# A hybrid decoder layer on one core: a third quarter-block product in the second map, with sums, residual and a gate on GpSimd

## The chip, the cores and the metric

The kernel runs on one core of a Trainium2 chip. The metric is the device time of one execution in microseconds (us). Engines are called as the profile calls them: PE (TensorE matmul) with PEld (its weight load), DVE (VectorE), ACT (ScalarE), POOL (GpSimd), SP (SyncE, which here only issues DMAs).

## The reference

One layer, in fp32, for a sequence of S = 2048 rows of width 1024 with hidden width 4096 (cut to what matters):

```python
h = x * (1.0 + sc1) + sh1
z = h @ w_in                       # 1024 x 2048
gate_b, gate_c, v_conv, v_pool = split(z)
mix = concat(gate_b * conv3(gate_c * v_conv), pool(v_pool)) @ w_out
x = layer_norm(ALPHA * x + (1.0 + g1) * mix, ln1_g, ln1_b)
h = x * (1.0 + sc2) + sh2
f = square(relu(h @ w_mlp_in)) @ w_mlp_out      # 1024 x 4096, 4096 x 1024
x = layer_norm(ALPHA * x + (1.0 + g2) * f, ln2_g, ln2_b)
```

The vectors sh1 to g2 come from a small product with c. The last two lines, called "second map" (the product with `w_mlp_out`) and "close" here, are where most of the change lies.

## The kernel before

The rows are cut into two blocks of T = 1024 rows. Each block passes through `in_proj`, `out_proj`, eight groups of `up` (the first MLP map, 512 hidden columns each, with squared ReLU), and `down` (the second map with the closing LayerNorm). The next stage's operands are made while the present one multiplies.

**Three passes per product.** fp32 operands are split by `split` (L80): ACT casts to a high part (L81), DVE subtracts it for a low part (L82), and `mm3` (L85) does three matmuls, high x high, high x low, low x high (L86 to L88).

**Seven products for eight.** Each large product is cut into 2 x 2 blocks and done with seven block products (Strassen-Winograd) on sums of blocks. `ORDER` lists the seven: 0 is A11 x B11, 1 is A12 x B21, 2 to 4 use sums on both sides, 5 and 6 a sum on one. The sums of blocks are made by DVE, go to DRAM (`usum`, `w2sum`) and come back as operands.

**`down` of block 2** (`b` = 1, L1082 on). F[0..7] are eight row tiles of 128 rows by 1024 columns of the result. A step is one block product over half of the hidden groups, so two steps make a product. The steps are `coarse = (0, 2, 3, 4, 6)`; each step has 96 matmuls of 128x512. `operands(n)` issues the loads and splits of a step while the step ahead of it runs. Products 1 and 5 are not in the list: they are "fine", that is each is once more cut into seven products of quarter blocks (256 columns wide, L1118), and these 14 follow step 1. The quarter sums come from `save_quarters` (activations, L960, made in `up`) and from `sum_blocks` on `w2q` (weights, `wquart`), both on DVE. Their loads need four transfers of 512 KB per quarter product.

**Order of the work.** A scheduler puts instructions into each engine's queue by the priorities in which the code issues them, and the tiles of a pool (`o` 12 buffers, `h` 28, `r` 5, `w` 6, PSUM `ps` 8 banks) hold a later user back until a buffer is free. GpSimd only issues stores.

**Residual.** `residual()` (L1066) makes ALPHA * ln1_g * n + ALPHA * ln1_b for eight tiles on DVE: load `nsave`, multiply, add, store to `rsave`. In block 2 it starts at step 2 (`base`), two tiles to a step.

**Close.** When a row tile is complete, `first_row` or `second_row` or `last` gates it with g2, adds the residual, and `normalise` does statistics, scale and finish. Product 3 ends the tiles 0 to 3 (`third_row`, where ACT copies PSUM into F), product 4 the right half of the tiles 4 to 7, product 6 their left half, which ends the kernel. The last row tile (F[7], left half) is done in two quarters of 256 columns in one PSUM bank (`cut` in `matmuls`), so that DVE can work on one while PE does the other. `last_part` gates a quarter by a DVE multiply out of PSUM, adds the residual and takes statistics.

**Start of `out_proj` of block 2.** `in_proj_1` ends with `keep` (L628, ACT copies out of PSUM), `conv` (ACT ACTIVATE L325, DVE L326, L327) and `pool_mid` (DVE L261, L265). The first matmuls of `out_proj` write into a PSUM bank that one of the L628 copies must have read.

Of the kernel before, what the change touches and what calls it, by code (L numbers as in the profile page):

```python
# [13 lines left out]
P = 128  # L14
# [17 lines left out]
QUARTER_SUMS = (0, 1, 1, 1, 1, 1, 1, 2)  # L32
# [11 lines left out]
def tile_hybrid_layer(ctx: ExitStack, tc: tile.TileContext, opening, xT, x, wada, vec, win0, win,  # L44
                      wins, wpool, wout, wmix, w1, w2, w2q, rows, out):
# [46 lines left out]


# [88 lines left out]
    uquart = tc.dram_tile([2, 7, 2, P, T], F32, name="uquart")  # L182
    wquart = tc.dram_tile([2, 2, 4, P, T], F32, name="wquart")
# [434 lines left out]

    def in_proj_1(X, W, first_w):
# [13 lines left out]

        def group(j):
# [6 lines left out]
            keep(cut(values, 0), x_)  # L641
            nc.vector.tensor_copy(v[:, :HALO], vhalo[:, j, :])
# [4 lines left out]
            add(cut(values, 0), y_)  # L647
            if j == 0:
                inputs(X, ORDER[4][1])
# [5 lines left out]
            keep(cut(values, 1), x_)  # L655
            if j == 0:
                inputs(X, ORDER[5][1])
            product(3, z_, True)
            keep(cut(gates, 1), z_)
            if j == 0:  # L660
                inputs(X, ORDER[6][1])
# [4 lines left out]
            add(cut(gates, 1), x_)  # L666
            if last:
                ops.begin(1)
            product(5, z_, False)
            add(cut(values, 1), z_)  # L670
            if last:
                ops.weights(0, 1)
                pt = pool_mid(1, j, v)
            product(6, x_, False)
            keep(cut(gates, 0), x_)
            if last:
# [6 lines left out]
            for hs in halves if last else [slice(0, T)]:  # L683
# [4 lines left out]
                if last and hs.start == 0:  # L688
                    mixed.extend([y[:, :H], None, pt[:, :H], pt[:, H:]])
# [267 lines left out]
    FINE = {1: 0, 5: 1}  # L957
    UQ = {"11": 0, "12": 1, "22": 2, "s1": 3, "s2": 4, "s3": 5, "s4": 6}

    def save_quarters(r, n, g):  # L960
        hf, cols = g // 4, slice(g % 4 * Q, g % 4 * Q + Q)
        a11, a21, a12, a22 = (r[:, i * Q : i * Q + Q] for i in range(4))
        q = t_o()
        s1, s2, s3, s4 = (q[:, i * Q : i * Q + Q] for i in range(4))
# [4 lines left out]
        tt(s1, a21, a22, ALU.add)  # L969
        tt(s2, s1, a11, ALU.subtract)  # L970
        tt(s3, a11, a21, ALU.subtract)
        tt(s4, a12, s2, ALU.subtract)
        nc.gpsimd.dma_start(dst[3:7].rearrange("a p n -> p a n"), q.rearrange("p (a n) -> p a n", a=4))

# [3 lines left out]
    def up(g, B, fine):  # L978
# [19 lines left out]

        def save(r, i):
            if fine and i in (1, 7):  # L1000
                save_quarters(r, i // 4, g)
            else:
                nc.gpsimd.dma_start(usum[g, i], r)  # L1003
# [466 lines left out]
```

## Time and profile before

| | |
|---|---|
| median of 3 runs | 1734.32 us (1734.28 to 1735.41) |
| profiled execution | 1734.73 us, span 1733.0 us |
| PE busy | 1720.9 us, 99% |
| PEld busy | 1439.4 us, 83% |
| DVE busy | 1342.6 us, 77% |
| ACT busy | 879.5 us, 51% |
| POOL busy | 235.7 us, 14% |
| granted TensorE clock, mean | 0.999 |

The span runs from the first to the last instruction of the core; the 1.73 us that the profiled execution has beyond it lie outside. A matmul's listed duration is longer than its pitch, since matmuls are pipelined: the distance between starts is what a matmul costs. Idle time of an engine other than PE matters only where PE, or the end, waits for it.

### The profile page before, as it was taken

To read this page: it belongs to the slowest core of one execution; us is meant where nothing else is said; L and a number is where in the kernel's file an instruction comes from. 1 tells how busy PE (TensorE), PEld (TensorE's weight loads), DVE (VectorE), ACT (ScalarE), POOL (GpSimd) and SP (SyncE) were. 2 spreads that over 40 slices of the span, in tenths; PEclk is the share of its full clock that TensorE was granted. 3 is DMA by queue.
4 is the path that set the end of the run, shared out by engine and by line. 5 is a ranking of instruction groups with operands and counts; after the bars stand their busy time and mean duration, and the time that the engine had idled before them with its cause. 6 is when DMAs were issued, how large, how long until landed. Compare 5 with 4: busy or idle time off the path is not lost.

```text
span 1733.0 us, 22349 instructions
## 1 busy us (share of the span) xinstructions
PE 1720.9 (99%) x7998; PEld 1439.4 (83%) x7998; DVE 1342.6 (77%) x1759; ACT 879.5 (51%) x1188; POOL 235.7 (14%) x441
## 2 busy tenths in 40 slices
PE   9999999999999999999999999999999999999997
PEld 8888888888888888888888888888888888998886
DVE  8898798877777676769686779687677768987894
ACT  5323358554454654436573344775444565763451
POOL 0222221122322000000000000103222221000000
PEclk9999999999999999999999999999999999999999
DMA  9899867778888998887572265657655599998871
GB/s 385 343 322 357 321 229 282 280 272 318 327 320 325 366 413 326 303 289 270 190 273 79 104 236 201 218 196 263 248 205 213 201 325 409 417 362 311 285 257 49
DMA packets 149646, 480.47 MB, mean 277 GB/s; under 512 B 17680, under 2 KB 18464, under 8 KB 149536
## 3 DMA queue, kind: packets, MB, share of 16 engines
q1 hardware_dynamic: 102528, 313.87, 49.8%
q0 software_dynamic: 47008, 165.19, 25.0%
q8 instruction: 62, 1.02, 0.2%
q14 instruction: 48, 0.39, 0.1%
HBM read 329.56 MB, written 149.43 MB: 276 GB/s over the span
## 4 chain that ended last, share of the span: by engine, by line
PE 95%; DVE 2%; issue 2%; DMA 1%; ACT 0%; POOL 0%; SPq 0%; DVEq 0%; POOLq 0%; ACTq 0%
PE ps L86 29%; PE ps L87 29%; PE ps L88 29%; PE ps L1118 5%; PE ps L406 3%; PE ps L757 1%; DVE o L91 1%; DMA r<-msum 1%; DMA msum<-o 0%; DMA r<-in_opening 0%; DVE o L1333 0%; DVE o L1339 0%; DVE o L261 0%; DVE st L726 0%; DVE h L82 0%
## 5 line engine op out<-in xcount | busy, mean ns | idle before, releaser
L87 PE MATMUL ps<-h,w 128*128 128x512 f32 x1312 | 510.3, 389 | 0.0
L88 PE MATMUL ps<-h,w 128*128 128x512 f32 x1312 | 510.1, 389 | 0.0
L86 PE MATMUL ps<-h,w 128*128 128x512 f32 x1312 | 510.1, 389 | 0.0
L86 PE MATMUL ps<-h,h 128*128 128x512 f32 (+1 forms) x1000 | 387.9, 388 | 2.2 <-DVE o L91 1.7
L88 PE MATMUL ps<-h,h 128*128 128x512 f32 (+1 forms) x1000 | 387.7, 388 | 0.0
L87 PE MATMUL ps<-h,h 128*128 128x512 f32 (+1 forms) x1000 | 387.5, 387 | 0.0
L81 ACT CAST h<-r 128x1024 fp32r<-128x1024 f32 (+1 forms) x196 | 199.4, 1021 | 279.0 <-PE ps L87 147.5
L82 DVE TENSOR_TENSOR h<-r,h 128x1024 fp32r<-128x1024 f32 (+1 forms) x196 | 230.9, 1182 | 83.4 <-ACT h L81 83.1
L81 ACT CAST w<-r 128x1024 fp32r<-128x1024 f32 x156 | 164.2, 1053 | 257.0 <-PE ps L87 251.2
L87 PEld LDWEIGHTS ps<-h,w 128*128 128x128 f32 x1312 | 246.3, 188 | 51.8 <-DVE h L82 0.5
L88 PEld LDWEIGHTS ps<-h,w 128*128 128x128 f32 x1312 | 246.3, 188 | 51.1
L86 PEld LDWEIGHTS ps<-h,w 128*128 128x128 f32 x1312 | 246.0, 188 | 51.4 <-issue 0.3
L82 DVE TENSOR_TENSOR w<-r,w 128x1024 fp32r<-128x1024 f32 x156 | 190.6, 1222 | 96.5 <-ACT w L81 95.5
L86 PEld LDWEIGHTS ps<-h,h 128*128 128x128 f32 x1000 | 187.8, 188 | 41.3 <-DVE o L91 1.9
L88 PEld LDWEIGHTS ps<-h,h 128*128 128x128 f32 x1000 | 187.8, 188 | 38.5
L87 PEld LDWEIGHTS ps<-h,h 128*128 128x128 f32 x1000 | 187.8, 188 | 38.0
L91 DVE TENSOR_TENSOR o<-o,o 128x1024 f32<-128x1024 f32 (+2 forms) x218 | 186.0, 859 | 42.8 <-DMA usum<-o 39.2
L82 DVE TENSOR_TENSOR h<-w,h 128x1024 fp32r<-128x1024 f32 x124 | 151.2, 1219 | 4.9 <-ACT h L81 4.8
L91 DVE TENSOR_TENSOR o<-o,ps 128x512 f32<-128x512 f32 (+1 forms) x172 | 112.4, 664 | 48.6 <-PE ps L88 48.2
L81 ACT CAST h<-w 128x1024 fp32r<-128x1024 f32 x124 | 130.0, 1049 | 9.5 <-DMA w<-in_w 4.3
L1003 POOL DMA_DIRECT2D usum<-o x96 | 51.7, 538 | 431.9 <-ACT o L997 195.8
L91 DVE TENSOR_TENSOR r<-r,r 128x1024 f32<-128x1024 f32 x60 | 73.4, 1223 | 11.4 <-DMA r<-in_w 7.6
(151 smaller groups left out, 1419.3 us busy)
## 6 DMA issues: line engine op xcount, KB each, us to landing
usum<-o POOLq DMA_DIRECT2D x96, 512.0 KB, 4.2
r<-usum SPq DMA_DIRECT2D x96, 512.0 KB, 5.3
w<-w2sum SPq DMA_DIRECT2D x64, 512.0 KB, 6.1
r<-in_w SPq DMA_DIRECT2D x60, 512.0 KB, 5.8
o<-in_w SPq DMA_DIRECT2D x72, 256.0 KB, 5.8
w2sum<-o POOLq DMA_DIRECT2D x64, 256.0 KB, 6.0
w<-in_w SPq DMA_DIRECT2D x32, 512.0 KB, 6.0
r<-uquart SPq DMA_DIRECT2D x28, 512.0 KB, 9.5
```

Of the source, the lines that this page charges most:

```text
L81: high = nc.scalar.copy(hi, src)
L82: return high.ins, nc.vector.tensor_tensor(lo, src, hi.bitcast(F32), op=ALU.subtract).ins
L86: nc.tensor.matmul(ps, whi, xhi, start=first, stop=False, skip_group_check=goes_on)
L87: nc.tensor.matmul(ps, whi, xlo, start=False, stop=False, skip_group_check=goes_on)
L88: nc.tensor.matmul(ps, wlo, xhi, start=False, stop=last, skip_group_check=goes_on)
L91: return nc.vector.tensor_tensor(out_, a, b_, op=op)
L406: nc.tensor.matmul(ps[m, h], wt[:, w : w + P], A[k][p // 2][:, hs], start=k == 0 and p == 0, stop=k == KD - 1 and p == 2)
L757: nc.tensor.transpose(ps[:, t * P : t * P + P], R[4 * h + t][:, k * P : k * P + P], ident)
L1003: nc.gpsimd.dma_start(usum[g, i], r)
L1118: nc.tensor.matmul(ps, a[:, us], w[:, gs], start=not begun, stop=hf == 1 and g == 3 and a is ul, skip_group_check=True)
```

## The change

- **Third fine product.** Product 0 of block 2's second map leaves `coarse` and becomes seven quarter products, ahead of those of 1 and 5. Product 2 is now the first coarse step and is the one that begins the banks X. Matmuls: 192 fewer of 128x512, 336 more of 128x256. Product 0's result is gathered in the left half of F[4..7], copied by ACT to the right half, and added to F[0..3] by DVE; X is added behind product 5.
- **Operands for it.** The blocks A11 of each group are quartered too (`save_quarters`), for the groups 0 and 1 on GpSimd from a copy that is read back (`again`), for the others on DVE. `save_quarters` now has pauses, and a `Spare` list spreads its pieces between the products of `up`.
- **Weights' quarter sums on GpSimd.** The sums of `w2q`, now of three sets, leave DVE and the end of each `up` group. GpSimd does them in 12 items of four TENSOR_TENSOR 128x512 each, with two loads and four stores on its own queue; four of the items in `in_proj_1`, eight in `up`. The input `w2s` is the same weights laid out for two loads of 128x1024.
- **Residual on GpSimd.** The 16 operations of block 2's residual go from DVE to GpSimd, and begin at step 0: one tile in each of the steps 0 and 1, three in step 2, two in step 3, one in step 4.
- **Product 6 in two.** Its first half ends the banks X. At the start of the second half DVE adds X to F, gates it and adds it to the residual (12 operations of 128x512). The second half runs into fresh banks with weights that GpSimd has multiplied by g2 (8 operations of 128x512), so a tile is closed by one sum (`close.sum`). Each quarter of the last row tile has a PSUM bank of its own.
- **Smaller.** `third_row` adds on DVE where ACT copied. In the last group of `in_proj_1` the pooling step is issued behind both halves' multiplies.

The diff, cut to its core:

```diff
+    def quarter_sums(n, hf, p):
+        a, b_ = t_o(T), t_o(T)
...
+        for i, r in enumerate((a, b_)):
+            nc.gpsimd.dma_start(r, w2s[n, hf, p, i])
+        yield
+        yield
+        gt(b22, b22, b12, ALU.subtract)
+        gt(b12, b12, b11, ALU.subtract)
+        yield
+        gt(b11, b22, b11, ALU.add)
+        gt(b21, b21, b11, ALU.subtract)
...
-                pt = pool_mid(1, j, v)
...
                 if last and hs.start == 0:
+                    pt = pool_mid(1, j, v)
...
-    FINE = {1: 0, 5: 1}
+    FINE = {0: 2, 1: 0, 5: 1}
...
+            for hs in halves if gate is not None else ():
+                nc.gpsimd.tensor_tensor(q[:, hs], q[:, hs], gate, op=ALU.mult)
...
-            tt(r, r, ag, ALU.mult)
-            tt(r, r, ab, ALU.add)
+            op = gt if ends[0] == 0 else tt
+            op(r, r, ag, ALU.mult)
+            op(r, r, ab, ALU.add)
             nc.gpsimd.dma_start(rsave[t], r)
-            if t % 2:
+            if t in ends:
                 yield
...
-        coarse = (0, 2, 3, 4, 6) if b else (0, 1, 2, 3, 5, 4, 6)
+        coarse = (2, 3, 4, 6) if b else (0, 1, 2, 3, 5, 4, 6)
...
             for c in range(0, H if cut else 0, Q):
+                ps = t_ps()
...
-                        mm3(banks[3][:, c : c + Q], uh[:, cs], ul[:, cs], wh[:, ws_], wl[:, ws_],
-                            False, n == len(ops) - 1 and p == 1, True)
-                last_part(slice(c, c + Q), banks[3][:, c : c + Q])
+                        mm3(ps[:, :Q], uh[:, cs], ul[:, cs], wh[:, ws_], wl[:, ws_],
+                            n == p == 0, n == len(ops) - 1 and p == 1)
+                last_part(slice(c, c + Q), ps[:, :Q])
...
         def third_row(t, ps):
-            keep(t + 4, hi_, ps)
+            add(t + 4, hi_, ps)
...
         def last_part(cs, ps):
-            tt(F[7][:, cs], ps, g2[:, cs], ALU.mult)
-            close.add(7, cs, rest[6][3][:, cs])
+            close.sum(7, cs, rest[6][3][:, cs], ps)
...
-        base = 2 if b else 5
+        base, turns = (0, 5) if b else (5, 4)
...
-        later = residual()
+        later = residual((0, 1, 4, 6, 7) if b else (1, 3, 5, 7))
...
+                if b and i == 6:
+                    for t in range(4):
+                        add(t + 4, lo_, X[t])
+                        gate(t + 4, lo_)
+                        tt(rest[6][t], rest[6][t], F[t + 4][:, lo_], ALU.add)
+                    table[6] = Y, True, last
...
+                        if k == 0:
+                            nc.scalar.copy(F[t + 4][:, hi_], F[t + 4][:, lo_])
+                            continue
+                        cs = lo_ if k == 1 else hi_
+                        tt(F[t][:, cs], F[t][:, cs], F[t + 4][:, lo_], ALU.add)
+                        if k == 5:
+                            add(t, hi_, X[t])
...
-            sums = [(sum_blocks, [w2q[n, i, hf] for i in range(4)], wquart[n, hf], p)
-                    for n in range(2) for hf in range(2) for p in halves]
```

Line numbers of the changed kernel differ: its DVE helper is L90 (L91 before), its GpSimd helper L94, a tile's scale L1454 (L1333), its finish L1460 (L1339), a quarter's statistics L1427 (L1309).

**The end of the kernel on DVE.** The rows below stand at the end of DVE's queue, from the scale of the row tile before the last (L1333) to the last tile's statistics; `o_11449` is the last row tile, `ps_11549` its one bank, `bc` the row of g2. Before:

```order
L1333 SCALAR_TENSOR_TENSOR o_14128<-o_11448,mv_14130,w_13402 128x1024
L91 TENSOR_TENSOR o_11449<-ps_11549,bc_4830 128x256
L1339 SCALAR_TENSOR_TENSOR o_14128<-o_14128,mv_14130,w_13404 128x1024
L91 TENSOR_TENSOR o_11449<-o_11449,r_14022 128x256
L1309 BN_STATS st_13789<-o_11449 128x6
```

After, with `o_11543` the last row tile and `r_14365` its residual:

```order
L1454 SCALAR_TENSOR_TENSOR o_14483<-o_11542,mv_14485,w_13732 128x1024
L90 TENSOR_TENSOR o_11543<-r_14365,ps_14496 128x256
L1460 SCALAR_TENSOR_TENSOR o_14483<-o_14483,mv_14485,w_13734 128x1024
L1427 BN_STATS st_14124<-o_11543 128x6
L90 TENSOR_TENSOR o_11543<-r_14365,ps_14523 128x256
L1427 BN_STATS st_14124<-o_11543 128x6
L789 BN_AGGR mv_14551<-st_14124 128x2
```

The multiply by g2 and the separate addition have become one sum from a quarter's own bank (`ps_14496`, `ps_14523`); the scale and the finish of the tile before stand as they did.

**The start of `out_proj` on ACT.** In ACT's queue, where the last group of `in_proj_1` ends; the L628 copies free PSUM banks, L325 is the first step of the convolution of one half. Before:

```order
L628 COPY o_8142<-ps_8059 128x512
L325 ACTIVATE o_8142<-o_8046,vecs 128x512
L628 COPY o_8143<-ps_8072 128x512
L325 ACTIVATE o_8142<-o_8046,vecs 128x512
L81 CAST h_8353<-o_8309 128x512
```

After, where the copies are L676 and the convolution L327:

```order
L676 COPY o_8194<-ps_8111 128x512
L327 ACTIVATE o_8194<-o_8098,vecs 128x512 x2
L676 COPY o_8195<-ps_8124 128x512
L80 CAST h_8395<-o_8413 128x512
L80 CAST h_8390<-o_8194 128x512
```

The second copy now stands behind both ACTIVATEs; these wait for two DVE multiplies, which now stand next to each other in DVE's queue, where a pooling step (L261) stood between them.

**The residual.** Before, in DVE's queue, while product 2's second step ends; `r_13202` and `r_13207` are two residual tiles, the L82 rows are splits of operands:

```order
L91 TENSOR_TENSOR r_13202<-r_13202,o_12884 128x1024
L91 TENSOR_TENSOR o_11445<-o_11445,ps_11549 128x512
L82 TENSOR_TENSOR h_13183<-r_13178,h_13182 128x1024
L82 TENSOR_TENSOR h_13187<-w_13180,h_13186 128x1024
L91 TENSOR_TENSOR r_13202<-r_13202,o_12886 128x1024
L91 TENSOR_TENSOR r_13207<-r_13207,o_12884 128x1024
```

After, the tiles 5 to 7 in POOL's queue, which in this stage holds nothing else:

```order
L94 TENSOR_TENSOR r_13690<-r_13690,o_11640 128x1024
L94 TENSOR_TENSOR r_13690<-r_13690,o_11642 128x1024
L94 TENSOR_TENSOR r_13695<-r_13695,o_11640 128x1024
L1178 DMA rsave<-r_13690 128x1024
L94 TENSOR_TENSOR r_13695<-r_13695,o_11642 128x1024
L1178 DMA rsave<-r_13695 128x1024
L94 TENSOR_TENSOR r_13942<-r_13942,o_11640 128x1024
```

The two operations of each tile and its store are now in one queue, and DVE's queue has the splits without the residual between them.

More of the change, by code (lines that the diff above doesn't have):

```diff
@@ L1033, in up @@
             join(c12, Z)
+            beside_()
+        for item in kept:
+            quarters_beside.finish(item)
         s1 = t_o()
@@ L1047, in up, with down_operands @@
         save(c11, 7)
-    def down_operands(i, gs):
+        beside_()
+        if fine and g == NC - 1:
+            quarters_beside.step(99)
+            sums_beside.step(99)
+    def down_operands(i, gs, gate=None):
         a, w = ORDER[i]
@@ L1064, in down_operands, with residual @@
         return out_, done
-    def residual():
+    def residual(ends):
         ag, ab = row(t_o(D), rows[0]), row(t_o(D), rows[1])
@@ L1123, in quarter_of @@
             c = (H if i == 5 else 0) + col * Q
-            return [F[2 * row + t][:, c : c + Q] for t in range(2)]
+            return [F[(0 if i else 4) + 2 * row + t][:, c : c + Q] for t in range(2)]
         def fine_copy(i, row, col, bank):
@@ L1146, in down, with matmuls @@
         fine_banks = {}
-        def matmuls(banks, ops, new, begins, ends, then, by_tile, cut=False):
+        def matmuls(banks, ops, new, begins, ends, then, by_tile, cut=False, closes=False):
+            begins = begins or cut
             if new and begins:
-                for t in range(4):
+                for t in range(3 if cut else 4):
                     banks[t] = t_ps()
```

135 lines of the change are left out of this document (106 added, 29 removed).

## The prediction

> **What bounds the kernel now.** I read the page's busy times and its chain first, then PE's waits over block 2, then the chain, the timelines and the table by stretches at the places that the change touches. Busy times and the shares of the chain:
>
> ```profile
> PE 1720.9 (99%) x7998; PEld 1439.4 (83%) x7998; DVE 1342.6 (77%) x1759; ACT 879.5 (51%) x1188; POOL 235.7 (14%) x441
> ...
> PE 95%; DVE 2%; issue 2%; DMA 1%; ACT 0%; POOL 0%; SPq 0%; DVEq 0%; POOLq 0%; ACTq 0%
> ```
>
> PE is the bound nearly everywhere, so two things can shorten the time: less matmul work, and the few places where PE stands still. PE's waits from 900 us to the end (line, what it waited for, total, times, longest) are two:
>
> ```profile
> PE ps L86 <- DVE o L91: 1.7, 1, 1.7
> PE ps L86 <- ACT o L628: 0.6, 1, 0.6
> ```
>
> The first lies at the end, the second at the start of `out_proj`. The end, from the timelines of DVE and PE (start, length, what, idle time before):
>
> ```profile
> 1717.20 0.69 DVE L91 TENSOR_TENSOR o<-ps,bc 128x512 f32<-128x512 f32 x1
> 1717.93 0.69 DVE L91 TENSOR_TENSOR o<-o,r 128x512 f32<-128x512 f32 x1
> ...
> 1720.04 1.27 DVE L1333 SCALAR_TENSOR_TENSOR o<-o,mv,w 128x1024 f32<-128x1024 f32 x1
> 1721.22 0.42 DVE L91 TENSOR_TENSOR o<-ps,bc 128x256 f32<-128x256 f32 x1
> ...
> 1724.87 0.42 DVE L91 TENSOR_TENSOR o<-ps,bc 128x256 f32<-128x256 f32 x1 [1.24 <-PE ps L88]
> 1725.32 0.42 DVE L91 TENSOR_TENSOR o<-o,r 128x256 f32<-128x256 f32 x1
> 1725.78 0.43 DVE L1309 BATCH_NORM_STATS2 st<-o 128x6 f32<-128x256 f32 x1
> ```
>
> ```profile
> 1719.76 0.28 PE L88 MATMUL ps<-h,h 128*128 128x256 f32 x1
> 1721.69 0.39 PE L86 MATMUL ps<-h,h 128*128 128x256 f32 x1 [1.66 <-DVE o L91]
> ```
>
> PE's second quarter of the last row tile (1721.69) writes the bank that DVE's multiply at 1721.22 still reads for the first quarter, and that multiply stood behind the scale of the tile before (1720.04). Then DVE waits for PE in turn, and from 1724.87 multiply, add, statistics, scales and finishes run alone to the end.
>
> **PE's work.** A matmul costs its pitch, not its listed length. The chain (start, length, what):
>
> ```profile
> 1400.09 0.23 PE ps L87
> ...
> 1406.21 0.23 PE ps L87
> ...
> 1467.87 80.63 PE ps L1118 x672
> ```
>
> The first two rows are the same line nine groups of three apart: 6.12 / 27 = 0.2267 us for 128x512. The third is the whole fine stage: 80.63 / 672 = 0.120 us for 128x256. The change takes away 192 of the first and adds 7 x 48 = 336 of the second: 336 x 0.120 - 192 x 0.2267 = 40.3 - 43.5 = **-3.2 us**. A half-wide matmul costs 53% of a full one, so seven products for eight (-12.5%) brings 7%.
>
> **The end.** With a bank for each quarter, PE's second quarter follows the first after 0.12 instead of 1721.69 - 1719.76 = 1.93 us: 1.81 less. Its result is then there at 1724.87 - 1.81 = 1723.06. Is DVE free by then? The tile before now has one sum where a multiply and an add stood, so all behind 1717.93 comes 0.73 earlier: its scale ends at 1721.31 - 0.73 = 1720.6; behind it stand quarter one's sum (0.42), the finish (1.27, as long as the scale) and quarter one's statistics (0.43), until 1722.7. It is free, with 0.4 us to spare. The last statistics start one sum of 0.45 later, at 1723.51 instead of 1725.78: **-2.27 us**.
>
> What pays for it are 12 operations of 128x512 on DVE at the start of the last step (add X, gate, add to the residual), 12 x 0.69 = 8.3 us. X's banks close six matmuls (1.36 us) apart, the last with the step's start; each brings 2.1 us of DVE work, so the four run from 4.1 us ahead of the step to 4.3 behind it, and the step's first tile comes after 24 x 0.2267 = 5.44 us. The cover is PE's first tile and an idle DVE (columns: stretch, length, then busy time and count of PE, PEld, DVE, ACT, POOL; clock, DMA share, GB/s):
>
> ```profile
> 1690.00:1712.00 22.00, 22.00 (x98) 18.21 (x97) 5.61 (x10) 1.18 (x4) 0.00 (x0) 1.00 0.00 1
> ```
>
> Without that cover the tiles would start up to 4 us late and regain 0.7 each. GpSimd's gate of the weights stands ahead of four splits in a stretch where DVE has time; I cost it at nothing there.
>
> **The start of `out_proj`.** ACT and DVE:
>
> ```profile
> 1043.89 0.73 ACT L325 ACTIVATE o<-o,vecs 128x512 f32<-128x512 f32 x1 [4.84 <-DVE o L91]
> 1044.52 0.57 ACT L628 COPY o<-ps 128x512 f32<-128x512 f32 x1
> ```
>
> ```profile
> 1042.02 1.23 DVE L261 TENSOR_TENSOR o<-o 128x1033 f32<-128x1033 f32 x1
> 1043.17 0.68 DVE L91 TENSOR_TENSOR o<-o,o 128x512 f32<-128x512 f32 x1
> ```
>
> PE's 0.6 us end with the copy, which stands behind the ACTIVATE, which waits for DVE's second multiply (1043.17) behind a pooling step of 1.23. With the multiplies adjacent that ACTIVATE starts 1.15 us earlier; the copy now stands behind a second one of 0.63 (1044.52 - 1043.89) that was behind it, so it comes about 0.5 earlier: **-0.5 us**, between 0 (the second half's pooling, now later, is waited for in its place) and -0.6.
>
> **DVE, ACT and the loads.** The third fine product is made at the pace of the other two. Two stretches of the fine stage, and the groups of ACT and DVE that feed it (count | busy, mean ns | idle before):
>
> ```profile
> 1468.00:1488.00 20.00, 20.00 (x169) 20.00 (x169) 18.45 (x18) 16.23 (x20) 0.00 (x0) 1.00 1.03 418
> ...
> 1528.00:1548.00 20.00, 20.00 (x169) 20.00 (x169) 17.96 (x19) 14.53 (x16) 0.00 (x0) 1.00 1.01 365
> ```
>
> ```profile
> L81 ACT CAST h<-r 128x1024 fp32r<-128x1024 f32 x28 | 29.5, 1052 | 16.2 <-PE ps L1118 15.6 <-DMA r<-uquart 0.6
> ```
>
> A quarter product takes 48 x 0.120 = 5.76 us and loads 2.1 MB, 364 GB/s; ACT's idle time ends with PE, which frees its buffers, so the preparation waits for PE and not the other way round. PE stayed full for 80 us at this pace, and 121 us are the same state for longer: 0, up to +2 if the 364 GB/s, with the residual's transfers now ahead of the stage, start with fewer buffers filled.
>
> In `up` DVE loses the weights' sums and gains quarter sums of activations. It is at 71% there:
>
> ```profile
> 1250.00:1300.00 50.00, 50.00 (x223) 41.39 (x222) 33.75 (x40) 23.26 (x28) 10.24 (x18) 1.00 0.60 222
> ```
>
> **GpSimd, and product 3.** The trace has no computation on POOL; how long its operations last, and whether they hold up DVE, is the open price. It matters where DVE is full:
>
> ```profile
> 1630.00:1650.00 20.00, 20.00 (x90) 16.57 (x89) 19.89 (x36) 13.28 (x27) 0.00 (x0) 1.00 0.71 239
> 1650.00:1670.00 20.00, 20.00 (x90) 16.57 (x89) 19.23 (x23) 10.89 (x16) 0.00 (x0) 1.00 0.96 349
> ```
>
> ```profile
> L91 DVE TENSOR_TENSOR o<-o,ps 128x512 f32<-128x512 f32 x8 | 5.5, 684 | 3.3 <-PE ps L88 3.2
> ...
> L91 DVE TENSOR_TENSOR r<-r,o 128x1024 f32<-128x1024 f32 x4 | 4.8, 1224 | 6.6 <-DMA r<-nsave 6.6
> ```
>
> ```profile
> 1655.73 1.21 DVE L82 TENSOR_TENSOR h<-w,h 128x1024 fp32r<-128x1024 f32 x1
> ```
>
> ```profile
> 1661.47 0.39 PE L87 MATMUL ps<-h,h 128*128 128x512 f32 x1
> ```
>
> The split that ends at 1656.94 is first used at 1661.47: a lead of 4.5 us, the shortest in this stage. From 1613 us the residual's four operations leave DVE (-4.9 us), `third_row` brings four adds of 0.68 (+2.7): the lead grows to 6.7. In the same stretch POOL now has six operations (residual tiles 5 to 7). If each stops DVE for a time d, PE loses 6d - 6.7 us: 0.6 at d = 1.22 (DVE's own length for the operation), 7.9 at twice that, nothing below 1.1. Some fall where DVE was idle anyway (the 6.6 above), and nothing in the trace shows that they stop DVE at all, so I take 0 and keep +8 for the range.
>
> The Trainium skill speaks against the change here: by "SBUF — State Buffer" (section "SBUF: two separate sides") GpSimd and a DVE operation with two SBUF inputs take one port pair in turn, each for its whole length, and by "GPSIMD Engine Reference" (section "3.1 Elementwise — side-by-side cycle accounting") an addition takes 4497 ns on GpSimd for 2048 elements, half of which, 2.25 us, is an estimate for 1024. By these d = 2.25 and the loss 6.8 us. No trace here shows either.
>
> **Sum.** -3.2 - 2.27 - 0.5 = -6.0. The profiled execution, 1734.73 (span 1733.0 and 1.73 outside it), becomes 1728.8; the median of the runs, 1734.32, lies 0.4 below it and becomes 1728.35. I forecast **1728.5**.
>
> **The rivals.**
> *GpSimd stops DVE for a while* (0.13). For it: DVE at 99% from 1630 on, nearly all of it with two SBUF inputs; against it, the lead of 6.7. With d between 1.5 and 2.7 the loss is 2.3 to 9.5 us and the time 1730.8 to 1738; at twice DVE's length, with two of the six in DVE's idle time, 4 x 2.44 - 6.7 = 3.1, thus 1731.6. This is the rule named above.
> *GpSimd is slow enough to make it slower* (0.12). The same place from d = 2.7 on, by stopping DVE, or because its residual tiles keep two of the five `r` buffers, behind which SP queues the loads of product 4. At three times DVE's length, 3.66, the loss is 15.3 us: 1743.8. For it: the loads and splits of a step have no other way in; against it: these loads are issued a step (96 x 0.2267 = 21.8 us) ahead of use.
> *The end doesn't do what it says* (0.10). DVE is late from the 12 operations, or another wait takes the bank's place. Then the 2.27 go, and with the 0.5 at `out_proj` in doubt too, only PE's 3.2 stay: 1734.32 - 3.2 = 1731.1. For it: only 0.4 us to spare at the last quarter, 1.1 at the first tile.
> *GpSimd's sums hold up `up`* (0.05). Each item takes two of twelve `o` buffers and stands in POOL's queue ahead of the stores that free the others; a late store makes ACT's copies and so PE wait. Against it: POOL is busy 10 of 50 us there. From a delay of some 9 us on; at 0.5 us in each of six groups 1731.5.
>
> **Numbers.** About 0.2%, 3.5 us, is what a measurement of this kernel can tell from no change: faster means below 1730.85, slower above 1737.8. My forecast has 0.60; its own range goes from 1727.3 (the `out_proj` term at 0.6, another 0.45 at the end, half a us of scatter, as 1734.28 to 1735.41 shows) to 1730.5 (+2 in the fine stage). It is faster with nearly all of its weight, and so is a third of the first rival: 0.64. Same: the rest of that rival, the third and the fourth: 0.24. Slower: 0.12. Up to 1735.5 the range holds the forecast, the third and fourth rival and about half of the first: 0.81.
>
> **What would show it.** Right: PE's waits lose both rows; the fine stage is one chain piece of 1008 matmuls, about 121 us long, at the same 0.120; the last statistics start 0.45 us behind PE's last quarter; POOL's operations lie beside DVE's splits without stretching them. Wrong: splits of 128x1024 that last longer than 1.22 us or start late while POOL computes; a wait of PE for DVE or ACT in the second half of product 3 or in product 4; a wait in the fine stage for `uquart` or `wquart`; PE idle in `up` behind ACT's copies; at the end, the first tile's sum behind the 12 operations.

## The result, and the profile after

The changed kernel takes 1766.59 us (median of 4 runs, 1763.7 to 1767.43), beside 1734.3 before (4 runs): a ratio of 1.0182, 95% interval 1.017 to 1.0194. It is 1.8% slower where 0.3% faster was forecast, and far outside the range. The page of the changed kernel, busy times and chain:

```profile
PE 1731.1 (98%) x8142; PEld 1449.5 (82%) x8142; DVE 1412.4 (80%) x1768; ACT 891.5 (51%) x1208; POOL 420.6 (24%) x581
...
PE 72%; DMA 9%; DVE 7%; POOL 4%; issue 4%; ACT 2%; SPq 0%; DVEq 0%; POOLq 0%; ACTq 0%
```

PE's share of the chain has gone from 95% to 72%, and DMA, DVE and POOL have come in. DVE, from which work was to be taken, is busy for 70 us more. PE's waits over the same stretch as in the prediction:

```profile
PE ps L87 <- DVE w L81: 10.6, 5, 4.0
PE ps L86 <- DVE h L81: 7.9, 3, 3.7
PE ps L85 <- ACT h L80: 2.1, 1, 2.1
PE ps L1219 <- ACT o L1229: 0.9, 1, 0.9
PE ps L85 <- DVE o L90: 0.6, 1, 0.6
PE ps L85 <- ACT o L676: 0.2, 1, 0.2
```

Both old waits have gone or shrunk (the 1.7 at the end, and 0.2 is left of the 0.6 at `out_proj`), and eleven new ones have come, eight of them for DVE's splits (L81). The quarter products mark the places (first and last start), in before and in after:

```profile
L1118 PE MATMUL ps<-h,h x672: 277/283/283, 1467.7 to 1548.2; 128*128 128x256 f32 x168
```

```profile
L1219 PE MATMUL ps<-h,h x1008: 278/283/386, 1485.3 to 1607.3; 128*128 128x256 f32 x168
```

They start 17.6 us later (0.5 earlier was forecast); about 1.0 of this is there before block 2 begins, because this execution's opening took 1.1 us longer. They last 122.0, where 80.5 and 336 more at 0.120 make 120.8: 1.2 lost. Behind them the span has 1764.1 - 1607.3 = 156.8, where 1733.0 - 1548.2 = 184.8 less two steps (43.5) and the 2.3 of the end make 139.0: 17.8 lost. With the 0.5, the sum of 37.1 is the whole distance from the forecast, half of it ahead of the quarter products and half behind.

Rows of the timelines, here and below, give start, length, engine, line, what, and in brackets the idle time before it and what ended that.

**Behind.** The timelines of POOL and DVE at the end of product 3 and the start of product 4 of the changed kernel:

```profile
1645.68 8.87 POOL L94 TENSOR_TENSOR r<-r,o 128x1024 f32<-128x1024 f32 x3 [13.27 <-DMA r<-nsave]
1654.48 0.60 POOL L1178 DMA_DIRECT2D rsave<-r  x1
1655.10 2.79 POOL L94 TENSOR_TENSOR r<-r,o 128x1024 f32<-128x1024 f32 x1
```

```profile
1648.08 1.37 DVE L1441 SCALAR_TENSOR_TENSOR o<-o,r 128x512 f32<-128x512 f32 x1 [0.85 <-DMA r<-rsave]
...
1649.38 2.88 DVE L1441 SCALAR_TENSOR_TENSOR o<-o,r 128x512 f32<-128x512 f32 x1
...
1652.19 0.68 DVE L90 TENSOR_TENSOR o<-o,ps 128x512 f32<-128x512 f32 x1
...
1652.91 2.71 DVE L90 TENSOR_TENSOR o<-o,bc 128x1024 f32<-128x1024 f32 x1
1655.55 3.42 DVE L1454 SCALAR_TENSOR_TENSOR o<-o,mv,w 128x1024 f32<-128x1024 f32 x1
...
1659.88 0.67 DVE L1441 SCALAR_TENSOR_TENSOR o<-o,r 128x512 f32<-128x512 f32 x1
```

While POOL computes (1645.7 to 1657.9), an operation of 0.67 us (1659.88, POOL idle) lasts 2.88, one of 1.22 lasts 2.71 and one of 1.28 lasts 3.42; the addition out of PSUM at 1652.19, in the midst of it, keeps its 0.68. A step earlier it was worse: while POOL did the six operations of the tiles 2 to 4 (1610.7 to 1631.5), six splits in a row lasted 2.9 to 3.4 us instead of 1.22. And something else hangs on GpSimd's tiles. The chain through this place (start, length, what):

```profile
1615.80 16.84 DVE h L81 x5
...
1636.22 9.32 DMA r<-nsave
...
1655.10 2.80 POOL r L94
...
1658.18 5.03 DMA rsave<-r
...
1663.27 3.50 DMA r<-usum
```

The residual's rows (`nsave`) are loaded late behind the stretched splits; GpSimd's operations and the store of their result follow; and only behind that store does SP's queue issue the loads of product 4's second step (`usum`, 1663.27). That step is due at 1672.8, so its four loads of `usum` come 9.5 to 1.6 us ahead; in the kernel before they came 32 to 18 us ahead (1625.3 to 1639.4 for 1657.2). Then PE runs dry, and its clock falls (columns as in the prediction):

```profile
1640.00:1660.00 20.00, 20.00 (x90) 16.55 (x89) 19.00 (x22) 4.48 (x8) 12.68 (x6) 1.00 0.71 276
1660.00:1680.00 20.00, 14.28 (x61) 11.34 (x60) 19.68 (x35) 12.48 (x29) 0.00 (x0) 0.95 0.89 336
1680.00:1700.00 20.00, 15.64 (x46) 11.44 (x46) 19.97 (x18) 11.50 (x16) 7.23 (x3) 0.62 0.84 292
```

From 1680 to 1700 PE is busy for 15.6 us, time for 69 matmuls at 0.2267, but does 46: the granted clock is 0.62. PE's rows there show it in the pitch:

```profile
1679.54 0.79 PE L86 MATMUL ps<-h,h 128*128 128x512 f32 x1 [3.58 <-DVE h L81]
1680.13 0.63 PE L87 MATMUL ps<-h,h 128*128 128x512 f32 x1
1680.56 0.63 PE L85 MATMUL ps<-h,h 128*128 128x512 f32 x1
```

0.43 us from start to start instead of 0.2267, until 1695: some 24 matmuls at 0.2 us more each, about 5 us behind the 10.1 of waits in this product.

**Ahead.** In `in_proj_1` PE waits 1.5 and 2.7 us for splits, behind the same kind of stretched operations: while GpSimd does sums (from 958 to 1003 us), a dozen of DVE's operations of 128x1024 last some 2.3 us. In `up` the two waits have another look; POOL, DVE and PE:

```profile
1321.60 0.57 POOL L660 DMA_DIRECT2D wquart<-o  x1 [0.30 <-POOL o L94]
1324.87 2.65 POOL L94 TENSOR_TENSOR o<-o,o 128x512 f32<-128x512 f32 x2 [2.69 <-DMA o<-in_w2s]
1327.46 0.56 POOL L660 DMA_DIRECT2D wquart<-o  x1
1328.04 1.30 POOL L94 TENSOR_TENSOR o<-o 128x512 f32<-128x512 f32 x1
1329.28 1.61 POOL L1081 DMA_DIRECT2D usum<-o  x3
```

```profile
1335.12 1.23 DVE L90 TENSOR_TENSOR o<-o,o 128x1024 f32<-128x1024 f32 x1 [10.14 <-DMA usum<-o]
```

```profile
1337.53 0.80 PE L87 MATMUL ps<-h,w 128*128 128x512 f32 x1 [3.95 <-DVE w L81]
```

Three stores of `usum` stand in POOL's queue behind GpSimd's operations, and these behind the load of `w2s`. DVE's next operation writes over a tile that one of these stores reads: it waits 10.1 us, with the next splits behind it, and PE waits 3.95.

**The end** went as forecast. DVE's last rows:

```profile
1756.20 0.42 DVE L90 TENSOR_TENSOR o<-r,ps 128x256 f32<-128x256 f32 x1 [0.52 <-PE ps L87]
1756.66 0.43 DVE L1427 BATCH_NORM_STATS2 st<-o 128x6 f32<-128x256 f32 x1
```

### The profile page after: what moved, and what is told of

The parts are those of the page before. It is cut to its first block, busy times and chain, and to the rows that moved or that the text cites. A ratio compares the mean times of both kernels' runs of the same rounds, so it can differ in the third digit from the quotient of the medians.

```text
span 1764.1 us, 22814 instructions
## 1 busy us (share of the span) xinstructions
PE 1731.1 (98%) x8142; PEld 1449.5 (82%) x8142; DVE 1412.4 (80%) x1768; ACT 891.5 (51%) x1208; POOL 420.6 (24%) x581
## 4 chain that ended last, share of the span: by engine, by line
PE 72%; DMA 9%; DVE 7%; POOL 4%; issue 4%; ACT 2%; SPq 0%; DVEq 0%; POOLq 0%; ACTq 0%
PE ps L85 21%; PE ps L87 21%; PE ps L86 21%; PE ps L1219 6%; PE ps L408 3%; DVE h L81 2%; POOL o L94 2%; DMA o<-in_w2s 2%; DVE o L90 2%; DMA usum<-o 2%; POOL r L94 1%; DMA r<-uquart 1%; PE ps L816 1%; DMA r<-nsave 1%; DVE w L81 1%
## 5 line engine op out<-in xcount | busy, mean ns | idle before, releaser
L86 PE MATMUL ps<-h,h 128*128 128x512 f32 (+1 forms) x936 | 365.2, 390 | 8.1 <-DVE h L81 7.9
L85 PE MATMUL ps<-h,h 128*128 128x512 f32 (+1 forms) x936 | 365.2, 390 | 3.0 <-ACT h L80 2.1
L87 PE MATMUL ps<-h,h 128*128 128x512 f32 (+1 forms) x936 | 364.7, 390 | 0.0
L80 ACT CAST h<-r 128x1024 fp32r<-128x1024 f32 (+1 forms) x202 | 205.5, 1021 | 264.7 <-PE ps L86 109.2
L81 DVE TENSOR_TENSOR h<-r,h 128x1024 fp32r<-128x1024 f32 (+1 forms) x202 | 251.6, 1250 | 79.9 <-ACT h L80 79.7
L81 DVE TENSOR_TENSOR w<-r,w 128x1024 fp32r<-128x1024 f32 x156 | 199.5, 1280 | 83.9 <-ACT w L80 83.3
L90 DVE TENSOR_TENSOR o<-o,o 128x1024 f32<-128x1024 f32 (+2 forms) x222 | 199.4, 905 | 51.4 <-DMA usum<-o 48.2
L86 PEld LDWEIGHTS ps<-h,h 128*128 128x128 f32 x936 | 176.9, 189 | 46.3 <-DVE h L81 10.3
L85 PEld LDWEIGHTS ps<-h,h 128*128 128x128 f32 x936 | 176.9, 189 | 40.6 <-ACT h L80 2.6
L87 PEld LDWEIGHTS ps<-h,h 128*128 128x128 f32 x936 | 177.0, 189 | 36.0
L81 DVE TENSOR_TENSOR h<-w,h 128x1024 fp32r<-128x1024 f32 x130 | 170.3, 1310 | 6.6 <-ACT h L80 6.5
L90 DVE TENSOR_TENSOR o<-o,ps 128x512 f32<-128x512 f32 (+1 forms) x182 | 117.6, 655 | 37.9 <-PE ps L87 32.9
L80 ACT CAST h<-w 128x1024 fp32r<-128x1024 f32 x130 | 136.4, 1050 | 15.6 <-POOL w L1157 6.8
L1219 PE MATMUL ps<-h,h 128*128 128x256 f32 x1008 | 121.4, 283 | 0.9 <-ACT o L1229 0.9
```

What stands on the lines that cost most here:

```text
L80: high = nc.scalar.copy(hi, src)
L81: return high.ins, nc.vector.tensor_tensor(lo, src, hi.bitcast(F32), op=ALU.subtract).ins
L85: nc.tensor.matmul(ps, whi, xhi, start=first, stop=False, skip_group_check=goes_on)
L86: nc.tensor.matmul(ps, whi, xlo, start=False, stop=False, skip_group_check=goes_on)
L87: nc.tensor.matmul(ps, wlo, xhi, start=False, stop=last, skip_group_check=goes_on)
L90: return nc.vector.tensor_tensor(out_, a, b_, op=op)
```

## The experiments

### What GpSimd's computation costs

**The changed kernel with its residual back on DVE.**

```diff
-            op = gt if ends[0] == 0 else tt
+            op = tt
```

> The changed kernel with the residual of block 2 back on DVE, at the changed kernel's places; all else as changed. In the changed kernel PE lost about 10 us of waits and some 7 us at a lower granted clock between 1660 and 1720 us, behind DVE operations that lasted 2.7 to 3.4 us instead of 1.2 while GpSimd computed residual tiles. Theory A (GpSimd's operations stop DVE operations that read two SBUF operands): most of this goes, 1747 to 1753 us. Theory B (the sums' loads and stores in POOL's queue, and with them late stores, are the cause): this stage has no such loads, so it stays above 1762. Theory C (product 3 is late because of third_row's four extra DVE adds and the earlier place of product 3): with 16 operations more on DVE it gets worse, above 1766.

Measured: 1753.55 us (2 runs), 13.0 less, at the upper edge of theory A's range. Behind the quarter products 1750.0 - 1605.7 = 144.3 us are left, 5.3 too many instead of 17.8: 12.5 go with GpSimd's residual. Theory C is out as the main cause: DVE has 16 operations more and PE waits less. But the run doesn't tell how much of the 12.5 is DVE being stopped and how much the late tiles: the loads of product 4's second step come earlier here too, 21 to 9 us ahead of it (1650.2 to 1662.0 for 1671.1).

**The kernel before with its residual on GpSimd** (`op` is GpSimd's helper in block 2), nothing else.

```diff
-            tt(r, r, ag, ALU.mult)
-            tt(r, r, ab, ALU.add)
+            op(r, r, ag, ALU.mult)
+            op(r, r, ab, ALU.add)
```

> The kernel before with one thing changed: the 16 residual operations of block 2 run on GpSimd, at their old places (two tiles to each step of products 2 and 3, the second step of which is DVE's full stretch). Theory A (GpSimd's operations stop DVE's operations on two SBUF operands): GpSimd needs some 3 us for each, DVE splits beside them last 2 us and more; the lead of 4.5 us before product 4 is used up and PE waits, 1736 to 1745 us. Rival (only the new order of product 3, right behind the quarter products, makes it late): DVE is relieved of 19.6 us and the time stays, 1733 to 1735.

Measured: 1738.48 us, ratio 1.002 (1.0009 to 1.003). Work taken off DVE makes the kernel slower. PE's waits:

```profile
PE ps L87 <- DVE h L82: 2.4, 3, 1.0
PE ps L86 <- DVE o L91: 1.7, 1, 1.7
```

The first row is new and lies in product 4, where the prediction had placed its rival. Here too both prices are paid: DVE's operations beside GpSimd's last up to 3.4 us, and DVE stands 3.6 us for a residual tile that GpSimd delivers late (until 1628.17).

**The kernel before with 28 additions on GpSimd that nobody needs**, in the quarter products.

```diff
+                    for _, (uh, ul, _, _) in enumerate(made[0]):
+                        nc.gpsimd.tensor_tensor(junk, uh[:, :H].bitcast(F32), ul[:, :H].bitcast(F32), op=ALU.add)
                     fine_product(k, part_, made.pop(0))
```

> The kernel before with 28 additions of 128x512 on GpSimd added in the quarter products (two to each, on operands that have just been split; their result is used by nobody). No queue, load or store depends on them. DVE is 91% busy there with operations on two SBUF operands and about 12 us ahead of PE. Theory A (such operations wait for each other): 28 x 1.35 = 38 us of DVE are lost, against 7 us idle and 12 us of lead, so PE waits some 15 to 20 us: 1745 to 1757. Without it: 1733 to 1736.

Measured: 1748.93 us, ratio 1.0083 (1.0063 to 1.0103). DVE's and POOL's groups in the quarter products (count | busy, mean ns | idle before):

```profile
L82 DVE TENSOR_TENSOR h<-r,h 128x1024 fp32r<-128x1024 f32 x27 | 54.9, 2035 | 0.0
L82 DVE TENSOR_TENSOR h<-w,h 128x1024 fp32r<-128x1024 f32 x28 | 36.1, 1290 | 0.0
L91 DVE TENSOR_TENSOR o<-o,ps 128x256 f32<-128x256 f32 x10 | 3.7, 407 | 0.0
L91 DVE TENSOR_TENSOR o<-o,ps 128x512 f32<-128x512 f32 x4 | 2.5, 675 | 0.0
```

```profile
L1275 POOL TENSOR_TENSOR tmp<-h,h 128x512 f32<-128x512 f32 x25 | 53.6, 2145 | 28.1 <-DVE h L82 27.9
```

DVE needs nothing from these operations; they read its splits, and each starts when a split of activations is ready. By reading them they keep buffers longer (ACT waits 3.5 us for that), but DVE is not idle ahead of any of these groups (0.0), so that is not what costs it time. Its splits of activations take 2.04 us instead of 1.22, those of weights, which alternate with them, 1.29, and the additions out of PSUM keep 0.41 and 0.68. GpSimd pays too: 2.1 us for an addition of 128x512 that lasts 1.3 when DVE leaves it alone (1328.04 above). That GpSimd's computing stops DVE, theory A, is shown here without any late store or load. The price is below the expected one: the splits lost 27 x 0.82 + 28 x 0.07 = 24 us, about three quarters of the 25 x 1.30 = 32 that the additions in this stretch would last alone, and PE waits 10.4 us.

### What the sums of the weights cost

**The changed kernel with `usum`'s stores on ACT's queue.**

```diff
-            nc.gpsimd.dma_start(usum[g, i], r)
+            (nc.scalar if fine else nc.gpsimd).dma_start(usum[g, i], r)
```

> The changed kernel with block 2's usum stores issued from ACT's queue instead of POOL's. In the changed kernel PE waits 3.95 and 1.87 us in up (about 11 us with the lower clock behind them), after DVE sat idle for 10.1 us until a usum store had read its tile. Theory B (stores stand behind GpSimd's waits for w2s loads and its operations in one queue): these waits go, 1754 to 1758 us. Theory A (DVE is stopped by GpSimd's operations): the waits stay, 1764 to 1768 us.

Measured: 1771.2 us. The waits in `up` fall from 5.8 us to 2.6, as theory B has it, but ACT's casts now stand behind stores that wait for DVE, and PE waits elsewhere instead (1.5 us in product 2, 3.6 at the first quarter products). The total is above the ranges of both theories and says nothing for either.

**The changed kernel with the sums back on DVE**, at the end of each `up` group.

```diff
-            some = HALF_SUMS[g]
+            some = (QUARTER_SUMS if b else HALF_SUMS)[g]
+QUARTER_SUMS = (0, 1, 2, 2, 2, 2, 2, 1)
...
-    for n_ in (2, 0, 1):
+    for n_ in ():
```

> The changed kernel with the quarter sums of the weights (three sets) back on DVE at the end of each up group, as before the change; residual, gate and the re-read quarters stay on GpSimd. Theories A and B both say that in_proj_1 (1.5 and 2.7 us of waits) and up (3.95 and 1.87) recover with their slow clock: 16 us less, 1749 to 1753 us. Theory C (the third quarter product itself is the burden): DVE has 33 us more in up and it stays at 1764 or more.

Measured: 1769.84 us, no gain, where both theories had 1749 to 1753. `in_proj_1` has no wait any more, as expected, but in `up` PE waits 6.7 and 1.0 us, and 4.7 at the first quarter products. The 6.7 begin as in the changed kernel: stores of `usum` behind GpSimd's sums of re-read quarters (3.4 us), DVE 7.5 us behind such a store, and then eight operations of sums ahead of the next split. Both theories had missed that sums on DVE, two halves to a group, come in bursts longer than the lead.

**The kernel before with the sums on GpSimd at their old place**, with their old loads on SP's queue (`quarter_blocks` is `sum_blocks` with GpSimd's helper).

```diff
-            sums = [(sum_blocks, [w2q[n, i, hf] for i in range(4)], wquart[n, hf], p)
+            sums = [(quarter_blocks, [w2q[n, i, hf] for i in range(4)], wquart[n, hf], p)
```

> The kernel before with one thing changed: the 32 operations of the weights' quarter sums (two sets) run on GpSimd, at their old places at the end of each up group; loads stay on SP's queue, stores on POOL's, where they were. Theory A alone: DVE is stopped for some 32 x 1.5 us in up, where it was idle 28% of the time: 1734 to 1738 us. Theory B (operations in POOL's queue hold back the stores of usum, and DVE waits for these before it may overwrite a tile): waits of DVE for a usum store of 5 us and more, and PE waits of 3 us and more in up, 1738 to 1750.

Measured: 1734.5 us, ratio 0.9998 (0.9988 to 1.0008). Splits beside them last 2.3 to 2.8 us instead of 1.22 here too, but DVE has the time, and PE never waits for it in `up`.

**The kernel before with the sums made the changed way**, in pieces, in `in_proj_1` and `up`, with loads on POOL's queue.

```diff
+        def beside_(j):
+            if 0 < j < NG - 1:
+                sums_beside.step()
```

> The kernel before with one thing changed: the weights' quarter sums of its two sets are made the changed way, on GpSimd in pieces between the products of in_proj_1 (four items) and up (four items), with loads and stores on POOL's queue. If in_proj_1 and up lose in the changed kernel because of these pieces: 6 us in in_proj_1 and 3 us or more in up, 1743 to 1750. If up lost because of the third set of quarters: 6 us in in_proj_1 alone, 1739 to 1742. If neither: 1734.

Measured: 1743.53 us. The quarter products start at 1475.0, 7.3 us later than before, all of it from `in_proj_1` (PE waits 0.9, 1.5 and 2.7 us); `up` has no wait. So `in_proj_1`'s loss comes from the pieces alone, and `up`'s only together with the third set (and the re-read quarters that come with it).

### Whether the third quarter product pays at all

**The changed kernel without computation on GpSimd**, in two ways: the quarters of A11 of the groups 0 and 1 at once, or read back and summed later.

```diff
-                sums_beside.items.insert(0, save_quarters(None, QUARTERED[i], g, True))
+                for _ in save_quarters(r, QUARTERED[i], g):
+                    pass
```

> The changed kernel with no computation on GpSimd at all: residual, weights' sums, re-read quarters and the gate of the weights on DVE. The third quarter product, the banks of the last tile and the closing by one sum stay. Theories A and B: what is left are the forecast's own terms, 1728 to 1733 us, unless DVE, now with some 60 us more than in the kernel before, is late somewhere. Theory C: 1740 or more.

> As the kernel with no computation on GpSimd, but the quarters of A11 of the groups 0 and 1 are read back and summed on DVE later in up, as the change places them, rather than at once in out_proj, where PE then waited 8.3 us at 1130 to 1156 us. If those waits were only this placing, 1735 to 1739 us: still 6 to 9 above the forecast, since PE waits 2.3 us in up, 2.5 in the first quarter products and 0.7 in product 3. If the third quarter product pays for itself, 1729 to 1732.

Measured: 1747.18 and 1746.4 us. The first loses 8.3 us of waits where `out_proj` ends and `up` begins and the quarters now stand; the second 9.7 in `up`, where DVE stands behind re-read tiles (one wait of 9.1 us) and bursts of sums. In the trace of before a split in `up` ends about 9 us ahead of its first use (one at 1410.1, used at 1419.2). Neither 1728 to 1733 nor, for the second, 1735 to 1739: where DVE's queue holds some 9 us of waits or extra work in one place, PE runs dry in both.

**Sums on GpSimd at the group's end, quarters from the tile itself, residual and gate on DVE;** and the same with a tile of its own for the last difference.

```diff
-            if fine and i in QUARTERED and (i or g > 1):
+            if fine and i in QUARTERED:
...
-        tt(c11, c21, c11, ALU.subtract)
-        save(c11, 7)
+        d21 = t_o()
+        tt(d21, c21, c11, ALU.subtract)
+        save(d21, 7)
```

> The changed kernel with residual and gate on DVE, the weights' sums on GpSimd at the end of each up group with loads on SP's queue (the way that cost nothing with two sets), and all quarters of A11 made on DVE from the tile itself in the following products, without re-reading. If DVE's bursts of sums and the waits for re-read tiles were what held up the third quarter product, up runs without waits of PE: 1731 to 1736 us. If the third set is too much for this stage whatever its place, PE waits 5 us or more in up: 1740 or more.

> As the kernel beside it (third quarter product, weights' sums on GpSimd at the group's end, residual and gate on DVE), and the last difference of an up group goes into a tile of its own instead of over one whose store is still reading. DVE then loses its waits for the usum store (22 us in up, 4 to 5 at the end of a group): 1729 to 1733 us if these waits are what leaves no room in up; the same as its neighbour if they hide nothing; slower if the thirteenth tile makes the twelve buffers short.

Measured: 1741.0 and 1741.41 us. `up` now runs without a wait (quarter products at 1468.5 in the first), and the fresh tile changes nothing. The loss is nearly all at the first quarter products: all of them take 130.0 us instead of 120.8 in the first of the two, and what follows is 1.1 too long. PE's waits of the first of the two, and ACT ahead of them:

```profile
PE ps L1221 <- ACT o L1231: 7.4, 1, 7.4
```

```profile
1458.47 1.06 ACT L1172 ACTIVATE o<-o 128x1024 f32<-128x1024 f32 x1 [8.14 <-DMA o<-in_rows]
```

ACT stands 8.1 us behind the residual's rows, with the casts for the quarter products behind it.

**The residual from product 3 on;** and the same with two halves of sums in each group from the second to the seventh.

```diff
-        base, turns = (0, 5) if b else (5, 4)
+        base, turns = (2, 3) if b else (5, 4)
...
-        later = residual((0, 1, 4, 6, 7) if b else (1, 3, 5, 7))
+        later = residual((3, 5, 7) if b else (1, 3, 5, 7))
```

> As the kernel with the third quarter product, the weights' sums on GpSimd at the group's end and all else on DVE, but the residual begins at product 3's first step (four tiles there, two in each of the next two) instead of at the first step of product 2. In its neighbour PE waited 7.4 us at the start of the quarter products, and 1.7 more went to the slow clock; ACT had stood 8.1 us behind the load of the residual's rows, with the casts for the quarter products behind it. If that early start of the residual is the cause, the wait goes: 1731 to 1733 us. If the loads of the third set themselves are late there (DMA engines full from 1430 us on), it stays: 1738 or more. New risk: 16 operations within product 3 and 4 on DVE, up to 3 us.

> As the kernel beside it, with the weights' sums two to a group from the second to the seventh group and none at the last, so that none of their loads and stores lie at the start of down. If the DMA engines at the start of the quarter products are what is short, this is faster than its neighbour, 1729 to 1732 us; if only the residual's early start was the cause, the same as its neighbour within 1 us.

Measured: 1733.16 us (1730.49 to 1735.81, 11 runs), ratio 0.9992 (0.9983 to 1.0001), and 1732.61 (10 runs), ratio 0.999 (0.9981 to 0.9999). The wait at the first quarter products has gone:

```profile
PE ps L87 <- DVE h L82: 1.1, 2, 0.7
PE ps L88 <- DVE w L82: 0.2, 1, 0.2
```

Nothing but the residual's place differs between the first of these and the kernel with 7.4, so its early start was the cause there, and the loads of a third set are not. The two are the same within what can be told.

### The terms of the forecast by themselves

**The kernel before with the change's end and its start of `out_proj`,** the gate on DVE, two quarter products.

```diff
+            for hs in halves if gate is not None else ():
+                nc.vector.tensor_tensor(q[:, hs], q[:, hs], gate, op=ALU.mult)
...
+                        tt(F[t + 4][:, lo_], X[t], g2[:, lo_], ALU.mult)
+                        tt(rest[6][t], rest[6][t], F[t + 4][:, lo_], ALU.add)
```

> The kernel before with the close and the start of out_proj of the change, without GpSimd: product 6 in two with the gate of its weights on DVE, a PSUM bank for each quarter of the last row tile, closing by one sum, and the pooling step behind both multiplies. Two quarter products as before, residual and sums on DVE. The forecast's terms say -2.3 and -0.5: 1731.5 us. Rival: another wait takes the place of the bank's, 1733.5 to 1734.5.

Measured: 1732.04 us (11 runs), ratio 0.9984 (0.9975 to 0.9993), 2.7 less. PE has no wait from 900 us on, and the last rows of DVE are:

```profile
1720.53 0.41 DVE L91 TENSOR_TENSOR o<-r,ps 128x256 f32<-128x256 f32 x1
1720.86 1.28 DVE L1354 SCALAR_TENSOR_TENSOR o<-o,mv,w 128x1024 f32<-128x1024 f32 x1
1722.05 0.42 DVE L1321 BATCH_NORM_STATS2 st<-o 128x6 f32<-128x256 f32 x1
1722.99 0.42 DVE L91 TENSOR_TENSOR o<-r,ps 128x256 f32<-128x256 f32 x1 [0.52 <-PE ps L88]
1723.44 0.43 DVE L1321 BATCH_NORM_STATS2 st<-o 128x6 f32<-128x256 f32 x1
```

The last statistics start at 1723.44 instead of 1725.78. It has the lowest median of the study, with nothing of the third quarter product and nothing on GpSimd; but the 0.6 between it and the last kernel above (0.9984 and 0.999, each within 0.0009) is less than the runs can tell.

## Why the prediction was wrong

- **PE's work, -3.2:** the pitch was right. In the last kernels above the 1008 quarter matmuls run at 0.120 (1467.5 to 1588.3 where PE never waits). The saving is real as work, but those kernels (1733.2 and 1732.6) don't come out below the one without it (1732.0): that the third quarter product shortens the time is not shown. In the profiled execution (1731.06) the part behind the quarter products takes 1729.3 - 1588.3 = 141.0 instead of 139.0, with waits of 1.1 in product 4; what brings other executions of the same kernel up to 1735.8 is not settled.
- **The end, -2.27:** right. Measured -2.34 at the last statistics in the kernel with the end alone, with the spare time at the last quarter (DVE done at 1722.5, PE's result at 1723.0) near the 0.4 forecast. The 12 operations were hidden: in the changed kernel too DVE waits 0.5 us for PE at the last quarter (1756.20).
- **`out_proj`, -0.5:** right in size: the wait fell to 0.2 in the changed kernel, and to nothing in the one with the end alone.
- **GpSimd and product 3, taken at 0: this step failed.** The prediction says: "nothing in the trace shows that they stop DVE at all, so I take 0". They do, and the part behind the quarter products is 17.8 us too long. The absence of a row was taken for a sign of absence, where the trace before could not have shown it. Two of the rivals were worked out for this very place, and both came: GpSimd stops DVE, and its slow residual tiles hold up the loads of product 4. The rivals' sum comes close, but partly by luck. The six operations last 2.8 to 3.4 us, 18.4 in all, which makes 18.4 - 6.7 = 11.7, and with the residual back on DVE 12.5 are regained. Yet DVE's operations beside these six grew by 10.7 only; the six of the tiles 2 to 4, a step ahead, which the prediction left out, had stretched six splits before; and the late loads and the clock of 0.62 come on top. The shares of these are not separated. Against the second rival stood that these loads are issued 21.8 us ahead of use; 9.5 and less were left.
- **The lead, 6.7:** too large as well. With the residual on DVE the same reckoning leaves 6.7 - 6 x 1.22 = -0.6, a loss of 0.6, but 5.3 are lost there. What the rest comes from is not settled; in the kernel with the residual from product 3 on it is 2.0.
- The Trainium skill had the mechanism: "SBUF — State Buffer" (section "SBUF: two separate sides") says that GpSimd and a DVE operation with two SBUF inputs hold one port pair in turn, each for its whole length. The trace agrees: 2.04 instead of 1.22 with two SBUF inputs, 0.68 and 0.68 with one in PSUM.
- By the Trainium skill, "GPSIMD Engine Reference" (section "3.1 Elementwise — side-by-side cycle accounting") the estimate for 1024 elements was 2.25 us; here the quickest of the residual's sixteen takes 2.41, the six in question 2.8 to 3.4 beside a busy DVE, and one of 512 alone takes 1.30.
- **`in_proj_1`, not in the sum: a step that was missing.** Four of the twelve items run there, and the lead was never looked up. In the kernel before they cost 7.3 us by themselves.
- **`up`, taken at 0:** wrong by about 11 (17.6 less the 6.7 that are there when `up` begins). The fourth rival had the queue right (stores behind GpSimd's operations), but looked for the harm in `o` buffers and ACT; it came through DVE, which overwrites a tile whose store is late. Its chance of 0.05 rested on POOL being busy 10 of 50 us, which says nothing of how long one item stands in front of one store. That the queue alone makes PE's waits is not shown: moving the stores to another queue halved them and made others. With the sums on GpSimd at the group's end and no re-read quarters they are gone.
- **The fine stage, 0 to +2:** the pace was right, 1.2 was lost at its start, and the reason was named: "the residual's transfers now ahead of the stage". The chain there goes through GpSimd's residual, the store of its tile (1486.11, 5.64 us) and the load of `uquart` that follows it. With the residual on DVE, but as early, 9.2 were lost (130.0 against 120.8), with ACT standing behind the load of the residual's rows, which no term had.

## What to carry to other kernels

Before work goes from DVE to GpSimd, add GpSimd's time to DVE's as an upper bound where DVE's operations read two SBUF operands (three quarters of it were lost beside the additions that nobody needs), and compare the sum with the shortest lead in that stage, not with DVE's average share. Then ask what waits for the moved work: it takes longer on GpSimd, so its result is later, with all that is queued behind it. A price that the profile of before cannot show is not zero: it belongs in the middle of the sum, or gets a small trial by itself. And in an in-order queue ask for each moved instruction what stands behind it; here a load, a sum and a row each held back something unrelated.

## What the runs showed of the hardware

- The stretching goes both ways: a GpSimd addition of 128x512 lasts 1.3 us alone and 2.1 beside DVE's splits; DVE's split of 128x1024 lasts 1.22 alone and, in that run, 2.04 for the activations and 1.29 for the weights. Beside GpSimd's operations of 128x1024 splits last up to 3.4.
- PE's clock can fall behind a wait: the pitch of 128x512 went from 0.2267 to 0.43 us, and 0.62 was granted over the 20 us that hold waits of 0.7 and 3.7 us and follow one of 3.6. The length of the wait alone does not decide it: in the changed kernel one of 1.9 (until 1380.67) was followed by 0.43 for 3.4 us, and one of 2.7 (until 1031.13) left 1.00 granted from 1020 to 1040. Four waits of 0.7 to 1.1 us, in the changed kernel with its residual on DVE, left 1.00 from 1650 to 1690.
- Waits of DVE for a store's read (19 us in all and at most 4.5 each, in the kernel with sums on GpSimd at the group's end) cost nothing where the lead of 9 us covered each of them; a fresh tile took them away and changed nothing.
